# Where the matmul operands lie modulo 512 bytes: moving the weight parts and the stationary arrays of a two-layer decoder trunk apart

## The chip, the core and the metric

The kernel runs on one core of one Trainium2 chip. The metric is the device time of one execution in microseconds (us). Of the kernel before there are three timed runs, and one more execution that the hardware profiler recorded; all numbers on where the time goes come from that one.

## What is computed

The reference is a decoder trunk of two layers over 256 tokens with 2048 features, all in float32. Cut to what matters here:

```python
hn = rms_norm(h, norm_mix[layer])
# layer 0: one input projection (2048 -> 6144), an RG-LRU group and an HGRN2 group, one output projection
# layer 1: q, k, v projection (2048 -> 6144), dilated attention over 16 heads, one output projection
h = h + mix
h = h + squared_relu_mlp(rms_norm(h, norm_mlp[layer]), mlp_w1[layer], mlp_w2[layer])  # 2048 -> 8192 -> 2048
...
return rms_norm(h, final_norm)
```

Nearly all of the arithmetic is matrix products of the 256 tokens with weights that are read once each.

## The kernel before, in words

**Two parts for each operand.** TensorE multiplies in a fast 32-bit format (float32r) that keeps fewer bits than float32. So each operand is split in two: `hi` is the value rounded to that format, `lo` is the rest. A product is three matmuls: hi with hi, hi with lo, lo with hi. The weights come in units of 128 x 2048 float32 (1 MB), by DMA into one of three `raw` buffers. `Weights.split` (L109) has ScalarE make `hi` by a copy (L112) and VectorE make `lo` by a subtraction (L113). There are three buffers each for `hi` and `lo` (pools `whi` and `wlo`, L49 and L50), taken in turn, so that unit n uses buffer n modulo 3, and the three units in flight overlap.

**The activations** are kept split as well, for all of the kernel or a stage of it: `bufa` (normed input, L62), `bufb` (mixed heads or hidden features, L259), `formx` and `formh` (sums and differences of blocks of `bufa` and `bufb`, for products that need seven instead of eight block products, L578 to L594 and L1036).

**The matmul loop.** In `tokens` (L311) and `blocks` (L605) the activation is the stationary operand, 128 x 128, loaded by a weight load (LDWEIGHTS), and a 128 x 512 piece of `hi` or `lo` moves past it. In `direct` (L230), used by layer 0's feature-major projections, it is the other way round: a 128 x 128 block of `hi` or `lo` is stationary, and 256 columns of `bufa` (or `bufb`) move. Every matmul has its own weight load, also where two in a row use the same stationary block. `mm` (L195) ties the matmuls into one fixed order, and `turn` (L198) sets transposes of float32 data into it. Loads of units run two units ahead of the products (`unit`, L185).

**Where arrays lie.** A pool takes a stretch of each partition of SBUF, on top of the pools opened before it; arrays follow each other in the order in which they are first asked for. `xall`, `bufa`, `raw`, `hi`, `lo`, `bufb`, `formx`, `formh`, `s` and `t1` all have sizes that are multiples of 512 bytes per partition, and what lies between them (`tmp`, 2560 bytes) is too. So all of them start at the same place modulo 512 bytes. Pieces that a matmul reads start at multiples of 512 bytes within them (128 or 512 columns of 4 bytes), so the moving and the stationary piece of every float32r matmul start at the same place modulo 512 too. Call the place of the stationary piece minus that of the moving one, modulo 512 bytes, the **distance**: before the change it is 0 throughout. Among the float32 matmuls there are other distances: transposes of `xall`, `y` and `as` by the identity (in `tab_`) have distance 0, those of `ho` have 192; `qT` (stationary) with `kT` has 0, and `xall` (stationary) with `pT` has 320.

Of the kernel before, what the change touches and what calls it, by code (L numbers as in the profile page):

```python
# [10 lines left out]
F32 = mybir.dt.float32  # L11
F32R = mybir.dt.float32r
# [8 lines left out]
P = 128  # L21
# [21 lines left out]
def trunk_kernel(ctx, tc, begin, xtok, cols, tab, masks, pos, fin, w_in, w_gate, w_out, w_qkv, w_o, w1, w2, out):  # L43
    nc = tc.nc
    pool = lambda name, bufs=1, **kw: ctx.enter_context(tc.tile_pool(name=name, bufs=bufs, **kw))
    cst = pool("cst")
    act = pool("act")
    wraw = pool("wraw", 3)
    whi = pool("whi", 3)  # L49
    wlo = pool("wlo", 3)  # L50
    tmp = pool("tmp", 2)
    mixers = ExitStack()
    pmm = pool("pmm", 3, space=PSUM)
# [27 lines left out]
    for step in ORDER.split():  # L81
        src, first, n = where[step[0]]
# [13 lines left out]
                    plan2(src, layer * 64 + q * 16 + 4 * n)  # L96
    at = [0, 0]

    behind, line = {}, []

    class Weights:
        def __init__(self, raw, step=2048, wait=(), follow=False):
            self.raw, self.wait, self.follow = raw, wait, follow
            self.hi = whi.tile([P, 2048], F32R, name="hi")
            self.lo = wlo.tile([P, 2048], F32R, name="lo")
            for at in range(0, 2048, step) if step else ():
                self.split(at, step)

# [95 lines left out]
    def put_off(wait, *fs):  # L204
        later.extend((clock[0] + wait, f) for f in fs)
# [369 lines left out]
    pairs, turned_ = ExitStack(), ExitStack()  # L575

    def open_pairs(layer):
        pool_ = pairs.enter_context(tc.tile_pool(name=f"pair{layer}", bufs=1))  # L578
        return pool_, pool_.tile([P, 4, 2, 512], F32R, name="formh")

    def part_forms(f, k, m, at, src):
# [8 lines left out]
        V.tensor_tensor(s4, a12, s2, OP.add)  # L590

    both = ctx.enter_context(tc.tile_pool(name="both", bufs=1))
    formx = both.tile([P, 4, 2, 512], F32R, name="formx")
    pair, formh = open_pairs(0)  # L594


# [6 lines left out]
    late = []  # L603
# [48 lines left out]
    def pair_forms(forms, k, src, z):  # L652
        h, l = (src[:, k:k + 2, c * S:c * S + S].bitcast(F32) for c in range(2))
        V.tensor_tensor(z.rearrange("p i j c -> p i (j c)"), h, l, OP.add)
        a11, a21, a12, a22 = (z[:, i, j] for i in range(2) for j in range(2))
        combos(a22, a11, a21, a12, a11, a21, a12, a22)
        part_forms(forms, k % 8 // 2, 1, slice(0, 4), z.rearrange("p i j (one c) -> p one (i j) c", one=1))
# [260 lines left out]
    def token_pair(i, c0, ready, raw=()):  # L918
        spare_ = wk.tile([P, 512], F32, name="q0", bufs=1) if not c0 and ATTENTION[:i].count("q") % 2 else None

        def out_(n, j):
            return xres[:, j, c0 + 512 * n:c0 + 512 * n + 512] if spare_ is None or (n, j) != (0, 0) else spare_

        def put(n, j, r=rt):
            def event(bank):
                with urgent():
                    if (n, j) in raw:
                        A.copy(out_(n, j), bank)
                    else:
                        A.activation(out_(n, j), bank, AF.Copy, scale=r[:, j:j + 1])  # L930
            return event

        def add(n, j, bank, r=rt):
            o = out_(n, j)
            with urgent():
                if (n, j) in raw:
                    V.tensor_tensor(o, bank, o, OP.subtract)
                else:
                    V.scalar_tensor_tensor(o, bank, r[:, j:j + 1], o, op0=OP.mult, op1=OP.add)

        def whole(n, j):
            if (n, j) in raw:
                with urgent():
                    A.activation(out_(n, j), out_(n, j), AF.Copy, scale=rt[:, j:j + 1])
            ready(n, j, out_(n, j))

        def final(n, j, bank):
            if (n, j) != (1, 0):
                put(n, j)(bank)
            else:  # L950
                add(n, j, bank)
            if (n, j) != (1, 1):
                whole(n, j)

        def u3(bank):
            add(1, 1, bank, rtn)
            whole(1, 1)

        blocks(w_qkv, 8 * i, 0, feature, formx,
               {"t2": put(1, 0, rtn), "t3": u3}, final)  # L960

    def queries_keys(i, raw=()):
        turned = [wk.tile([P, 4, S], F32, name="qT", bufs=1), wk.tile([P, 4, S], F32, name="kT", bufs=1)]

        def ready(n, j, o):
            t = o.rearrange("p (h c) -> p h c", h=4)
            r = t[:, :, :32].rearrange("p h (two c) -> p h two c", two=2)
            per = lambda a: a[:, j][:, None, :].to_broadcast([P, 4, 16])
            with urgent():
                b = wk.tile([P, 4, 2, 16], F32, name="rb", bufs=2)  # L970
                c = wk.tile([P, 4, 2, 16], F32, name="rc", bufs=2)
                V.tensor_tensor(b[:, :, 0], r[:, :, 1], per(sinT[:, 0]), OP.mult)
                V.tensor_tensor(b[:, :, 1], r[:, :, 0], per(sinT[:, 1]), OP.mult)
                V.tensor_tensor(c, r, cosT[:, j][:, None, None, :].to_broadcast([P, 4, 2, 16]), OP.mult)
                V.tensor_tensor(r, c, b, OP.add)

            def turns():
                p = psc.tile([P, 4, P], F32, name="pl", bufs=2)
                for h in range(4):
                    turn(p[:, h], t[:, h])  # L980
                with urgent():
                    A.copy(turned[n][:, :, j * P:j * P + P], p)

            put_off(WAIT_Q, turns)

        token_pair(i, 0, ready, raw)
        return turned
# [30 lines left out]
    def mix(hd, st):  # L1018
        vs = slice(D // 2 + (hd % 8) * P, D // 2 + (hd % 8) * P + P)
        po = psc.tile([P, S], F32, name="pd" if hd % 2 else "po", bufs=1)  # L1020
        mm(po, xres[:, 0, vs], st[:, :S], start=True, stop=False, skip_group_check=True)
        mm(po[:, P:], xres[:, 1, vs], st[:, S:], start=False, stop=True, skip_group_check=True)
        z = tmp.tile([P, S], F32, name="z")
        with urgent():
            A.copy(z, po)
        split_to(mixed(hd), z)
# [3 lines left out]
    for i, what in enumerate(ATTENTION):  # L1030
        if what == "v":
            token_pair(i, D // 2, lambda *_: None)
            if hd == 16:
                assert len(ready_) == 8
                mixers.close()
                late.append(pairs.enter_context(tc.tile_pool(name="forms1", bufs=1)).tile(  # L1036
                    [P, 8, 512], F32R, name="formh"))
            put_off(2, *(lambda h=h: mix(h, ready_.pop(h)) for h in range(hd - 8, hd)))
            if hd == 8:
                put_off(EARLY, *(lambda k=k: pair_forms(early_forms, k, bufb, wk.tile(  # L1040
                    [P, 512], F32, name="q0", bufs=1).rearrange("p (i j c) -> p i j c", i=2, j=2))
                    for k in range(0, 8, 2)))
        else:
            q, k = queries_keys(i, ((1, 0),) if not i else ())
            for h in range(4):
                put_off(WAIT_Q + 1 + 2 * h, head(hd, q[:, h], k[:, h], WAIT_S))
                hd += 1
# [141 lines left out]
```

## Time and profile before

| | |
|---|---|
| timed runs (3) | median 2133.09 us, 2132.8 to 2133.53 |
| the profiled execution's own time | 2133.06 us |
| its span, first to last instruction | 2131.3 us |
| matmuls, weight loads | 10542 each |
| busy: DVE (VectorE), ACT (ScalarE) | 1788.8 us, 1378.2 us |
| HBM read, mean rate over the span | 482.78 MB, 228 GB/s |

The profile names engines PE (TensorE's matmuls), PEld (its weight loads, which run beside matmuls), DVE, ACT, POOL (GpSimd) and SP (SyncE, which issues most DMAs). A row such as `L196 PE MATMUL p<-hi,bufa 128*128 128x512 f32 x1488 | 482.0, 394 | 0.0` says: line 196 of the kernel, output tile `p`, moving operand `hi`, stationary operand `bufa`, 1488 matmuls, busy 482.0 us in all, 394 ns for one, and 0.0 us of idle time ahead of them. Matmuls overlap in the pipeline, so 394 ns is a latency. What a matmul costs in a stream is the distance in time from its start to the next one's start, and that is read from the timeline or from the chain of work.

### The profile page before, as it was taken

Reading aid. Unit: us, or ns where it says so; the run is one execution under the profiler, and the core shown is the slowest. Engines: PE = TensorE matmul, PEld = TensorE weight load, DVE = VectorE, ACT = ScalarE, POOL = GpSimd, SP = SyncE. Lnnn points to the kernel's source line nnn. Section 1 sums busy time; section 2 is a strip of 40 time slices with the busy share of each in tenths; the row PEclk is TensorE's granted clock in tenths of the full one; section 3 lists DMA queues with packets and bytes.
Section 4 is the critical chain, followed back from the end, with each engine's and each line's share of the span. In section 5 each row is a group of like instructions: output and inputs, shape, how many; then the busy total and the mean of one; then the engine's idle time right before and its main releaser. Section 6 shows DMA issues by size and latency. Waiting matters only on the chain.

```text
span 2131.3 us, 26730 instructions
## 1 busy us (share of the span) xinstructions
PE 2120.9 (100%) x10542; PEld 1797.6 (84%) x10542; DVE 1788.8 (84%) x1962; ACT 1378.2 (65%) x1543; POOL 66.8 (3%) x85
## 2 busy tenths in 40 slices
PE   9999999999999999999999999999999999999998
PEld 8989998888888888888888888888888888888886
DVE  7777888888888888888988797788897888888887
ACT  7445565776476567567666777776756765755764
POOL 0000000000000000000000000000000000000000
PEclk9999999999999999999999999999999999999999
DMA  8444446686777677677887767777767768777773
GB/s 336 162 162 158 161 148 224 206 269 233 227 237 253 230 240 253 227 241 231 270 279 218 241 199 247 254 247 228 246 237 253 236 212 269 238 234 227 271 225 146
DMA packets 69806, 488.71 MB, mean 229 GB/s; under 512 B 7808, under 2 KB 8320, under 8 KB 11952
## 3 DMA queue, kind: packets, MB, share of 16 engines
q1 hardware_dynamic: 58176, 410.96, 51.1%
q0 software_dynamic: 11216, 75.70, 18.3%
q8 instruction: 82, 1.34, 0.3%
q14 instruction: 44, 0.36, 0.0%
q10 hardware_dynamic: 288, 0.34, 0.0%
HBM read 482.78 MB, written 4.19 MB: 228 GB/s over the span
## 4 chain that ended last, share of the span: by engine, by line
PE 99%; DVE 0%; ACT 0%; DMA 0%; issue 0%; ACTq 0%; DVEq 0%; POOLq 0%
PE p L196 62%; PE po L196 14%; PE pd L196 13%; PE pt L196 5%; PE pl L199 2%; PE pl L470 1%; PE pl L196 0%; PE pd L199 0%; DMA ppi<-in_pos 0%; PE pd L454 0%; DVE lo L113 0%; ACT hi L112 0%; PE pl L465 0%; PE po L495 0%; PE po L496 0%
## 5 line engine op out<-in xcount | busy, mean ns | idle before, releaser
L113 DVE TENSOR_TENSOR lo<-raw,hi 128x2048 fp32r<-128x2048 f32 (+2 forms) x397 | 787.1, 1991 | 164.5 <-ACT hi L112 159.4
L112 ACT CAST hi<-raw 128x2048 fp32r<-128x2048 f32 (+2 forms) x397 | 657.3, 1671 | 335.1 <-PE p L196 175.5
L196 PE MATMUL p<-hi,bufa 128*128 128x512 f32 x1488 | 482.0, 394 | 0.0
L196 PE MATMUL p<-hi,bufb 128*128 128x512 f32 x1128 | 363.1, 391 | 0.0
L196 PEld LDWEIGHTS p<-hi,bufa 128*128 128x128 f32 x1488 | 279.2, 188 | 57.3 <-DVE bufa L245 0.5
L113 DVE TENSOR_TENSOR lo<-s,hi 128x2048 fp32r<-128x2048 f32 (+1 forms) x164 | 285.9, 1753 | 28.6 <-ACT hi L112 27.6
L112 ACT CAST hi<-s 128x2048 fp32r<-128x2048 f32 (+1 forms) x164 | 242.7, 1480 | 98.2 <-DVE s L164 54.2
L196 PE MATMUL p<-lo,bufa 128*128 128x512 f32 x744 | 287.6, 390 | 0.2 <-DVE lo L113 0.2
L196 PEld LDWEIGHTS p<-hi,bufb 128*128 128x128 f32 x1128 | 211.7, 188 | 43.7
L196 PE MATMUL p<-lo,bufb 128*128 128x512 f32 x564 | 219.5, 389 | 0.0
L196 PE MATMUL p<-bufa,hi 128*128 128x256 f32 x1024 | 193.2, 287 | 0.0
L196 PEld LDWEIGHTS p<-lo,bufa 128*128 128x128 f32 x744 | 139.9, 188 | 28.0 <-DVE lo L113 0.7
L196 PEld LDWEIGHTS p<-bufa,hi 128*128 128x128 f32 x1024 | 161.2, 191 | 0.2
L196 PE MATMUL p<-bufa,lo 128*128 128x256 f32 x512 | 146.5, 286 | 0.0
L112 ACT CAST hi<-t 128x2048 fp32r<-128x2048 f32 x41 | 78.5, 1914 | 99.6 <-PE p L196 91.1
L113 DVE TENSOR_TENSOR lo<-t,hi 128x2048 fp32r<-128x2048 f32 x41 | 94.0, 2292 | 55.4 <-ACT hi L112 55.0
L196 PEld LDWEIGHTS p<-lo,bufb 128*128 128x128 f32 x564 | 105.9, 188 | 21.5
L196 PE MATMUL p<-hi,formh 128*128 128x512 f32 x368 | 120.7, 391 | 0.0
L196 PE MATMUL p<-hi,formx 128*128 128x512 f32 x352 | 115.9, 390 | 0.0
L196 PE MATMUL po<-hi,bufb 128*128 128x512 f32 x320 | 103.7, 390 | 0.0
L196 PEld LDWEIGHTS p<-bufa,lo 128*128 128x128 f32 x512 | 98.0, 191 | 0.0
L164 DVE TENSOR_TENSOR s<-s,raw 128x1024 f32<-128x1024 f32 x82 | 96.4, 1216 | 0.1
(319 smaller groups left out, 3292.4 us busy)
## 6 DMA issues: line engine op xcount, KB each, us to landing
raw<-in_w SPq DMA_DIRECT2D x224, 1024.0 KB, 6.1
raw<-in_w_in SPq DMA_DIRECT2D x44, 1024.0 KB, 4.8
raw<-in_w_qkv SPq DMA_DIRECT2D x42, 1024.0 KB, 6.9
t<-in_w SPq DMA_DIRECT2D x32, 1024.0 KB, 4.9
t<-in_w POOLq DMA_DIRECT2D x32, 1024.0 KB, 8.7
s<-in_w POOLq DMA_DIRECT2D x17, 1024.0 KB, 8.4
raw<-in_w_out SPq DMA_DIRECT2D x15, 1024.0 KB, 4.8
raw<-in_w_o SPq DMA_DIRECT2D x14, 1024.0 KB, 7.7
```

The source lines that it names most:

```text
L112: a = A.copy(h, w)
L113: v = V.tensor_tensor(l, w, h.bitcast(F32), OP.subtract)
L164: V.tensor_tensor(s, s, held["c"][:, at:at + 1024], OP.add)
L196: chain[:] = [after(T.matmul(*args, **kw), chain)]
L199: chain[:] = [after(T.transpose(out_, in_, ident), chain)]
L470: T.matmul(pl[:, j], kq[:, js], halves(qp[:, js], c, True), start=True, stop=True)
```

## The change

The change moves no instruction and adds none. It adds small arrays that nothing reads or writes, and takes the weight parts from one pool instead of two.

- The pools `whi` and `wlo` become one pool `parts`. Unit n takes `hi{n % 3}` and `lo{n % 3}` there, each with one buffer. Behind each of the three pairs lies an unused array `apart` of 16 floats, 64 bytes.
- `gap2` (48 floats, 192 bytes) lies ahead of `formx`, `gap3` and `gap4` (64 bytes each) ahead of the two homes of `formh`.

Counted from `bufa`'s place modulo 512 bytes, the arrays then lie as follows (before: all at 0):

| array | place after | distance to hi/lo of pair 0, 1, 2, as stationary |
|---|---|---|
| `bufa`, `raw`, `xall` | 0 | `bufa`: 0, 448, 384 |
| `hi0` `lo0`, `hi1` `lo1`, `hi2` `lo2` | 0, 64, 128 | to a moving `bufa`: 0, 64, 128 |
| `bufb` | 192 | 192, 128, 64 |
| `formx`, `s`, `t1` | 384 | `formx`: 384, 320, 256 |
| `formh` | 448 | 448, 384, 320 |

The distance stays 0 only where `bufa` meets pair 0.

```diff
-    whi = pool("whi", 3)
-    wlo = pool("wlo", 3)
+    parts = pool("parts")
...
-    behind, line = {}, []
+    behind, line, turns = {}, [], [0]
...
             self.raw, self.wait, self.follow = raw, wait, follow
-            self.hi = whi.tile([P, 2048], F32R, name="hi")
-            self.lo = wlo.tile([P, 2048], F32R, name="lo")
+            n = turns[0]
+            turns[0] += 1
+            self.hi, self.lo = (parts.tile([P, 2048], F32R, name=f"{part}{n % 3}") for part in ("hi", "lo"))
+            if n < 3:
+                parts.tile([P, 16], F32, name=f"apart{n}")
...
         pool_ = pairs.enter_context(tc.tile_pool(name=f"pair{layer}", bufs=1))
+        pool_.tile([P, 16], F32, name="gap3", bufs=1)
...
     both = ctx.enter_context(tc.tile_pool(name="both", bufs=1))
+    both.tile([P, 48], F32, name="gap2", bufs=1)
...
-                late.append(pairs.enter_context(tc.tile_pool(name="forms1", bufs=1)).tile(
+                forms1 = pairs.enter_context(tc.tile_pool(name="forms1", bufs=1))
+                forms1.tile([P, 16], F32, name="gap4", bufs=1)
+                late.append(forms1.tile(
                     [P, 8, 512], F32R, name="formh"))
```

## The prediction

> **What bounds the kernel now.** I read the page first: busy times, the clock row, and the shares of the chain of work that ended last.
>
> ```profile
> span 2131.3 us, 26730 instructions
> ...
> PE 2120.9 (100%) x10542; PEld 1797.6 (84%) x10542; DVE 1788.8 (84%) x1962; ACT 1378.2 (65%) x1543; POOL 66.8 (3%) x85
> ...
> PEclk9999999999999999999999999999999999999999
> ...
> PE 99%; DVE 0%; ACT 0%; DMA 0%; issue 0%; ACTq 0%; DVEq 0%; POOLq 0%
> ```
>
> TensorE works from end to end, at the full granted clock, and the chain is 99% its own. Next comes the view of who waited for whom, for the engines that make the weight parts.
>
> ```profile
> ACT hi L112 <- PE p L196: 269.1, 142, 4.3
> DVE lo L113 <- ACT hi L112: 242.0, 300, 3.8
> ```
>
> ScalarE waits for TensorE to give a buffer back (269.1 us in 142 waits), VectorE waits for ScalarE. The makers are ahead; TensorE sets the time. So only the distance from one matmul's start to the next one's can change the time by much. The chain in order of time gives it for long streams (start, length, count):
>
> ```profile
> 552.07 13.60 PE p L196 x60
> ...
> 2089.95 13.60 PE p L196 x60
> ```
>
> 13.60 us / 60 = 226.7 ns for a matmul of 512 moving columns, the same at both ends of the kernel. For 256 columns the timeline of layer 0's projections gives a stretch of 21 matmuls:
>
> ```profile
> 60.03 0.40 PE L196 MATMUL p<-bufa,hi 128*128 128x256 f32 x2
> ...
> 62.55 0.40 PE L196 MATMUL p<-bufa,hi 128*128 128x256 f32 x2
> ```
>
> (62.55 - 60.03) / 21 = 120.0 ns. So 256 more columns cost 226.7 - 120.0 = 106.7 ns, and a fixed 226.7 - 2 x 106.7 = 13.3 ns is left per matmul, for both lengths. This fixed part is all that the change can win; nothing else on TensorE's path depends on where arrays lie.
>
> **The change, part by part.** It moves places and no work: no DMA, cast, subtraction or matmul is added or dropped, and no queue is passed. Three things could cost or bring something.
>
> *1. The turn of the buffers.* Unit n still waits for unit n - 3, as with three buffers of one name. I cost it at nothing. What hides it is ScalarE's lead above: it would have to lose more than its waits for TensorE, up to 4.3 us each, before TensorE noticed. The bounds: if the new names gave another order of instructions, TensorE could wait a few times; by that longest wait, one or two of these are 4 to 9 us, and as TensorE hardly waits now, less than nothing is no gain. I take 0.
>
> *2. ScalarE and VectorE read and write at other places.* Their instructions have slack, as shown. Taken: 0.
>
> *3. The distance between moving and stationary piece.* Each matmul runs while the next one's stationary block is loaded. Before, the two reads start at the same place modulo 512 bytes, always; after, only `bufa` with pair 0 does. How many matmuls is that? The groups by shape and tile:
>
> ```profile
> L196 PE MATMUL p<-hi,bufa 128*128 128x512 f32 x1488 | 482.0, 394 | 0.0
> L196 PE MATMUL p<-hi,bufb 128*128 128x512 f32 x1128 | 363.1, 391 | 0.0
> ...
> L196 PE MATMUL p<-bufa,hi 128*128 128x256 f32 x1024 | 193.2, 287 | 0.0
> ...
> L196 PE MATMUL p<-hi,formh 128*128 128x512 f32 x368 | 120.7, 391 | 0.0
> L196 PE MATMUL p<-hi,formx 128*128 128x512 f32 x352 | 115.9, 390 | 0.0
> ...
> L196 PE MATMUL pt<-lo,formh 128*128 128x512 f32 x8 | 3.1, 389 | 0.0
> ```
>
> The 36 groups between the first and the last of these that hold `hi` or `lo` add up to 9,588 matmuls: 4,824 with `bufa`, 2,700 with `bufb`, 1,056 with `formx`, 1,008 with `formh`. A third of `bufa`'s meet pair 0 and keep distance 0. The distance changes for 9,588 - 4,824 / 3 = 7,980.
>
> What a changed distance costs, the trace doesn't show for float32r, as all of these are at distance 0. The bounds:
>
> - *Best:* the whole fixed part is the two reads in each other's way and goes away: 7,980 x 13.3 ns = 106 us less.
> - *Worst:* the fixed part grows. The nearest row is a stretch that follows four transposes, where the stream is out of its usual step:
>
> ```profile
> 379.45 0.60 PE L199 MATMUL pl<-tab__199,xall 128*128 128x128 f32 x4
> 379.81 0.48 PE L196 MATMUL po<-hi,formh 128*128 128x512 f32 x1
> 380.12 0.40 PE L196 MATMUL po<-lo,formh 128*128 128x512 f32 x1
> ...
> 382.44 0.39 PE L196 MATMUL po<-hi,formh 128*128 128x512 f32 x1
> ```
>
>   Ten matmuls from 380.12 to 382.44 take 2.32 us, 232.0 ns each, 5.3 ns over the settled 226.7. Same columns, same arrays; only the step of load and stream differs. If the new distances kept the stream out of step throughout: 7,980 x 5.3 ns = 42 us more.
> - *Nearest rows with another distance:* float32 matmuls. Transposes by the identity load a stationary block at distance 0 (`y`, `xall`) or 192 (`ho`); `qT` with `kT` is at 0, `xall` with `pT` at 320:
>
> ```profile
> L199 PE MATMUL pl<-tab__199,y 128*128 128x128 f32 x256 | 33.1, 272 | 0.0
> ...
> L199 PE MATMUL pl<-tab__199,xall 128*128 128x128 f32 x152 | 22.6, 272 | 0.0
> ...
> L196 PE MATMUL pl<-kT,qT 128*128 128x256 f32 x32 | 9.6, 380 | 0.0
> ...
> L508 PE MATMUL pt<-tab__199,ho 128*128 128x128 f32 x16 | 4.1, 273 | 0.0
> ...
> L196 PE MATMUL po<-pT,xall 128*128 128x256 f32 x16 | 4.7, 377 | 0.0
> ```
>
>   272 and 272 ns at distance 0, 273 at 192; 380 at distance 0, 377 at 320. A distance of 0 costs 1 ns less in one pair and 3 ns more in the other.
>
> I take 0 for the distance, as the rows with another distance are nearest to it and disagree in sign. A fixed part that is equal for 256 and 512 columns also looks like a cost of changing over from one stationary block to the next. I keep both ends for the range.
>
> One page of the Trainium skill speaks against any gain: "TensorE: Matmul & The Clock Gate", section "Part 2: What happens when you issue a matmul", says that TensorE has two independent read ports into SBUF, so that loading the next weights takes nothing from the running matmul; by that rule the sum is 0. The trace can't show it, as it has no float32r matmul at another distance.
>
> *The sum:* the profiled execution's own 2133.06 us (span 2131.3 and 1.8 around it) + 0 + 0 + 0 = **2133.1 us**, which is also the median of the three runs within 0.03 us.
>
> **The rivals.**
>
> *Slower: the stream doesn't settle.* For: the interval does depend on how load and stream stand to each other (232.0 against 226.7 ns), and the settled step was found at distance 0, one constant distance from matmul to matmul and from unit to unit. After, the distance jumps with each pair, that is every 12 to 24 matmuls, about as long as settling took above. Against: nothing shows that places and not only times make the step. Price: 2133.1 + 42 = 2175 us if no stretch at a new distance settles; if it settles half-way through each unit, 2154. It decides for slower as soon as the mean interval at new distances is over 227.2 ns (0.2% of 2133, 4.3 us, over 7,980).
>
> *Faster: the fixed part is a collision at equal places.* For: each matmul pays 13.3 ns beyond its columns, and `kT` with `qT`, at distance 0, takes 3 ns more than `pT` with `xall`. Against: the transposes show nothing, and a load and a stream that read at different speeds pass through all distances anyhow. Price: 2133.1 - 106 = 2027 us in full, 2080 for half of it. Nothing else would be late then: VectorE's 1788.8 us of work still fit under 2027. The same page's section "Back-to-back issue gap" gives columns / 2.4 + 2.5 ns for a matmul, 215.8 for 512 columns, where this trace measures 226.7. If the 10.9 ns between them were the collision, the gain would be 7,980 x 10.9 ns = 87 us and the time 2046; that is an estimate from the page's figure.
>
> *The change does nothing:* arrays that nobody uses might be given no space, or the reads may be arbitrated by something coarser or finer than 64 bytes. Then the time is 2133.1 too, and it belongs to the forecast.
>
> **How the numbers follow.** 0.2% is 4.3 us, about what a measurement of this kernel can tell from no change. Within 0.2%: 0.40, the likeliest, so the predicted time is 2133.1 us, and its own range is 2129 to 2137. Slower: 0.34, as the trace proves that the step of load and stream matters and that other steps than the settled one cost more; its times are spread from 2138 to 2185. Faster: 0.26, from 2027 to 2128. As the cases of both signs hold more than half, the range reaches into both: to 2085 (a gain of 48 us, somewhat under half of the best; 0.09 lies below) and to 2180 (a little over the full price of the unsettled stream; 0.07 lies above).
>
> **What would show it.** In the profile of the changed kernel, the chain in order of time has the streams of 60 matmuls: 13.60 us means the forecast, about 13.9 the unsettled stream, 13.0 or less the collision. The mean would not say which distance does it: the intervals at `bufa` with pair 0 must stay at 226.7 ns whatever the others do, and if a distance matters, the stretches of one pair with one array differ from each other in the timeline. If ScalarE's waits for TensorE have shrunk while TensorE shows idle time at `lo` or `hi`, the turn of the buffers was costed wrongly. The prediction is wrong if the streams of 60 have another length; it is right for a wrong reason if gains at some distances cancel losses at others.

## The result, and the profile after

The changed kernel takes 2160.56 us (median of 4 runs, 2160.49 to 2161.39), the kernel before 2132.95 us (4 runs): a ratio of 1.0132, interval 1.012 to 1.0144, 27.6 us more. The page of the changed kernel:

```profile
span 2159.6 us, 26730 instructions
...
PE 2148.1 (99%) x10542; PEld 1796.2 (83%) x10542; DVE 1789.8 (83%) x1962; ACT 1377.9 (64%) x1543; POOL 66.8 (3%) x85
...
PEclk9999999999999999999999999999999999999999
...
PE 98%; ACT 1%; DVE 1%; DMA 0%; issue 0%; SPq 0%; ACTq 0%
```

As many instructions as before, the same work on DVE and ACT within 1 us, the same clock, and the span 28.3 us longer. TensorE still makes up nearly the whole chain. ScalarE's waits for TensorE have grown a little, from 269.1 us; the makers of the weight parts are still ahead (the view of waits of the changed kernel):

```profile
ACT hi L114 <- PE p L198: 283.4, 160, 4.3
DVE lo L115 <- ACT hi L114: 263.6, 322, 3.9
```

So TensorE's matmuls follow each other more slowly. The chain of the changed kernel in order of time (start, length, count), where 60 matmuls took 13.60 us before:

```profile
596.75 13.90 PE p L198 x60
...
766.53 13.71 PE p L198 x60
...
1066.47 13.97 PE p L198 x60
```

They take 228.5 to 232.8 ns each now, and differ from stream to stream. The timeline shows what they go by. Units take pairs 0, 1, 2 in turn, so each stretch has one pair and one array. Starts at the ends of three stretches in the changed kernel (columns: start, length, what):

```profile
383.43 0.40 PE L198 MATMUL p<-lo,bufb 128*128 128x512 f32 x1
...
388.55 0.39 PE L198 MATMUL p<-hi,bufb 128*128 128x512 f32 x1
388.78 0.39 PE L198 MATMUL p<-hi,formh 128*128 128x512 f32 x1
...
391.58 0.39 PE L198 MATMUL p<-hi,bufb 128*128 128x512 f32 x1
...
396.85 0.39 PE L198 MATMUL p<-hi,bufb 128*128 128x512 f32 x1
```

- `bufb` with pair 1, distance 128: 22 matmuls in 5.12 us, 232.7 ns each.
- `formh` with pair 2, distance 320: 12 in 2.80 us, 233.3 ns.
- `bufb` with pair 0, distance 192: 23 in 5.27 us, 229.1 ns.

Layer 0's matmuls of 256 columns, where `bufa` moves past `hi` or `lo`, went the other way at one distance:

```profile
60.03 0.40 PE L198 MATMUL p<-bufa,hi 128*128 128x256 f32 x2
...
63.51 0.28 PE L198 MATMUL p<-bufa,lo 128*128 128x256 f32 x1
...
68.45 0.28 PE L198 MATMUL p<-bufa,lo 128*128 128x256 f32 x1
```

Pair 0, distance 0: 29 matmuls in 3.48 us, 120.0 ns as before. Pair 1, distance 64: 42 in 4.94 us, 117.6 ns.

Taken over all float32r matmuls, each one's time from start to next start in the changed kernel minus that of the same matmul in the kernel before, added up by distance modulo 256:

| distance | 512 columns: matmuls, us more | 256 columns: matmuls, us more |
|---|---|---|
| 0 | 1416, 1.6 | 576, -0.2 |
| 64 | 1560, 9.9 | 432, -1.3 |
| 128 | 2640, 13.6 | 624, -0.6 |
| 192 | 2339, 5.5 | none |

The sum is 30.6 - 2.1 = 28.5 us; all other matmuls give -0.1 us, so this is the whole of the span's 28.3 but for rounding. Why modulo 256, and whether distance or something that goes with it does this, is what the experiments are for.

### The profile page after: what moved, and what is told of

It is laid out like the page before. It is cut to its first block, busy times and chain, and to the rows that moved or that the text cites. A ratio compares the mean times of both kernels' runs of the same rounds, so it can differ in the third digit from the quotient of the medians.

```text
span 2159.6 us, 26730 instructions
## 1 busy us (share of the span) xinstructions
PE 2148.1 (99%) x10542; PEld 1796.2 (83%) x10542; DVE 1789.8 (83%) x1962; ACT 1377.9 (64%) x1543; POOL 66.8 (3%) x85
## 4 chain that ended last, share of the span: by engine, by line
PE 98%; ACT 1%; DVE 1%; DMA 0%; issue 0%; SPq 0%; ACTq 0%
PE p L198 62%; PE po L198 14%; PE pd L198 13%; PE pt L198 5%; PE pl L201 2%; PE pl L472 1%; PE pl L198 0%; DMA first<-in_begin 0%; PE pd L201 0%; PE pd L456 0%; ACT hi L114 0%; DVE lo L115 0%; ACT L227 0%; DVE xc L549 0%; ACT gi L227 0%
## 5 line engine op out<-in xcount | busy, mean ns | idle before, releaser
L198 PE MATMUL p<-hi,bufb 128*128 128x512 f32 x1128 | 367.7, 394 | 0.0
L198 PE MATMUL p<-hi,formx 128*128 128x512 f32 x352 | 117.6, 395 | 0.0
```

Of the source, the lines that this page charges most:

```text
L198: chain[:] = [after(T.matmul(*args, **kw), chain)]
```

## The experiments

Theory A: the time from one matmul to the next is set by the distance between the stationary and the moving piece. Theory B, the prediction's slower rival: distances as such cost nothing, but a jump of the distance unsettles the stream. All kernels below are one edit of the kernel before or of the changed one. Intervals that are called means are of all matmuls of a kind in a trace, those next to float32 matmuls (over 260 ns, or over 160 ns at 256 columns) left out.

**Other steps** (`e1_probe32`), an edit of the changed kernel:

```diff
-                parts.tile([P, 16], F32, name=f"apart{n}")
+                parts.tile([P, 8], F32, name=f"apart{n}")
...
-    both.tile([P, 48], F32, name="gap2", bufs=1)
+    both.tile([P, 16], F32, name="gap2", bufs=1)
```

> The same edit with half of the steps: pairs at 0, 32, 64 bytes, bufb at 96, formx at 160, formh at 224. Theory A (the interval between matmuls is a function of the distance between the stationary and the moving piece modulo 256 bytes, whatever the arrays): at distances 64, 128 and 192 the same intervals as in the changed kernel, 233.4, 232.2 and 229.5 ns, now with other arrays; the new distances 32, 96, 160 and 224 lie between their neighbours, about 230, 233, 231 and 228 ns, and the time is about 2155 us. Theory B (a jump of the distance from pair to pair unsettles the stream, whatever the distance): jumps as often as in the changed kernel, so about 2160 us and intervals that do not depend on the distance.

2167.29 us (2 runs), against 2132.8 for the kernel before: slower than either theory said. Means with `bufb` at 64: 233.2 ns; with `formx` at 128: 232.9; with `formh` at 192: 230.0, so other arrays at the known distances have the known intervals within 0.6 ns. The new ones do not lie between their neighbours: 233.0 at 32, 233.8 at 96, 233.8 at 160, 233.1 at 224. Distance matters, and 0 is a narrow dip.

**One constant distance of 64** (`e2_all64`), an edit of the kernel before:

```diff
+    pool("ahead").tile([P, 48], F32, name="ahead")
     whi = pool("whi", 3)
     wlo = pool("wlo", 3)
+    pool("behind").tile([P, 16], F32, name="behind")
```

> The kernel before with 192 bytes ahead of the weight parts and 64 behind them: every stationary array now lies at one and the same distance, 64 bytes modulo 256, from every pair, so nothing jumps. Theory A: 233.4 ns in place of 227.2 for some 7825 matmuls of 512 columns, 48 us more, less up to 6 us in layer 0's matmuls of 256 columns: about 2177 us, 2168 to 2185. Theory B: no jumps, so 2133 us.

2177.56 us, ratio 1.021 (1.0195 to 1.0225). In the chain of this kernel all such streams take 14.00 or 14.01 us:

```profile
556.74 14.00 PE p L198 x60
598.74 14.00 PE p L198 x60
```

14.00 / 60 = 233.3 ns, with no jump anywhere. Theory B falls as the only cause: a constant distance of 64 costs more than the changed kernel's jumps.

**A distance of 256** (`e3_bufa256`): as above, with 64 floats ahead of `whi` and none behind.

> The kernel before with 256 bytes ahead of the weight parts: bufa now lies at distance 256 from every pair, bufb, formx and formh stay at 0. Theory A (period 256): 2133 us, within 4 us. Rival C (period 512, so that 256 is a distance like the others, with 2 to 6 ns more for bufa's 3203 intervals): 2139 to 2153 us. Theory B: 2133 us.

2133.21 us, ratio 1.0002 (0.9992 to 1.0012), streams as in the kernel before:

```profile
550.99 13.60 PE p L197 x60
```

The period is 256 bytes, not 512. It also shows that what moved with `hi` and `lo` (their distance to `raw`, 256 bytes) does no harm.

**The gaps alone** (`e4_gaps`): the changed kernel without the steps between pairs.

```diff
     parts = pool("parts")
+    pool("behind").tile([P, 48], F32, name="behind")
     tmp = pool("tmp", 2)
...
-            if n < 3:
-                parts.tile([P, 16], F32, name=f"apart{n}")
```

> The changed kernel without the steps between the pairs: all three pairs at 0, bufb at 192, formx at 384, formh at 448 as there. The distance is constant for each array. Theory A: bufb 2580 x 2.5 ns, formx 1042 x 5.3 ns, formh 1000 x 2.5 ns, 14.5 us in all: about 2147.5 us, 2143 to 2152, with bufa at its old interval. Theory B: only the changes from array to array are left, 2133 to 2138 us.

2147.11 us, ratio 1.0067 (1.0052 to 1.0082), 14.3 us more where theory A had 14.5 us. Modulo 512, `hi`, `lo` and `raw` lie here where they were, and of the operands only the stationary arrays have moved. The streams, `bufb` at 192 and `formh` at 448:

```profile
552.50 13.73 PE p L197 x60
```

13.73 / 60 = 228.8 ns. `bufa`, at distance 0 throughout, has a mean of 228.1 here and 227.5 in the kernel before.

**The pairs alone** (`e8_pairs`): the changed kernel without the three gaps, and with an `apart2` that puts `bufb` back to 0.

```diff
-                parts.tile([P, 16], F32, name=f"apart{n}")
+                parts.tile([P, 16 if n < 2 else 96], F32, name=f"apart{n}")
...
-        pool_.tile([P, 16], F32, name="gap3", bufs=1)
...
-    both.tile([P, 48], F32, name="gap2", bufs=1)
...
-                forms1.tile([P, 16], F32, name="gap4", bufs=1)
```

> The other half of the change: pairs at 0, 64 and 128 as in the changed kernel, bufb, formx and formh back at 0. Theory A: every array now meets distances 0, 192 and 128 in turn, 2.8 ns more on average for some 7825 matmuls, 22 us, less 2.6 us in the 256-column ones: about 2152 us, 2148 to 2157, so that the two halves, 14.3 us (gaps alone) and this, add up to more than the whole's 27.6. Rival F (the halves cost each for itself): 27.6 - 14.3 = 13.3 us, 2146 us.

2157.42 us, ratio 1.0112 (1.0097 to 1.0128), against 2133.21: 24.2 us more, at the upper edge of theory A. The two halves add up to 38.5 us where the whole costs 27.6, so rival F falls: a distance is a difference, and moving both sides can bring them back together. What theory A missed by 5 us is in the third of the matmuls that are at distance 0. With `bufb` they take 229.1 ns here and 227.0 ns in the kernel before. The timeline shows why; this unit of `bufb` with pair 0 starts at 554.12, behind one of `formh` at another distance:

```profile
554.35 0.40 PE L198 MATMUL p<-lo,bufb 128*128 128x512 f32 x1
...
556.43 0.39 PE L198 MATMUL p<-lo,bufb 128*128 128x512 f32 x1
...
559.15 0.39 PE L198 MATMUL p<-lo,bufb 128*128 128x512 f32 x1
```

Nine matmuls in 2.08 us, 231.1 ns each, then 12 in 2.72 us, 226.7 ns each: coming from another distance, the stream needs part of the unit to settle. So the jumps do cost something, at distance 0.

**The source of the parts** (`e7_raw64`), an edit of the kernel before:

```diff
+    pool("ahead").tile([P, 16], F32, name="ahead")
     wraw = pool("wraw", 3)
+    pool("behind").tile([P, 48], F32, name="behind")
```

> The kernel before with raw moved: 64 bytes ahead of the raw buffers and 192 behind them, so that raw lies 64 bytes (modulo 256) from the hi and lo that are made of it, while hi, lo and all stationary arrays stay at distances of 0 or 256 from each other. Theory A: 2133 us, within 4 us. Rival D (the places that ScalarE and VectorE read and write while TensorE reads are what counts): another time, 10 us or more away, as in the changed kernel.

2132.78 us, ratio 0.9999 (0.999 to 1.0008), and the streams stay:

```profile
551.49 13.60 PE p L198 x60
592.29 13.60 PE p L198 x60
```

Rival D falls for the casts' source. ScalarE's casts do not feel the places either; here they are in the kernel before (first row), in this one (second) and in the changed one (third), with minimum, median and maximum in ns after the count:

```profile
L112 ACT CAST hi<-raw x397: 604/1912/1927, 21.5 to 2106.3; 128x2048 fp32r<-128x2048 f32 x144, 128x1024 fp32r<-128x1024 f32 x54, 128x512 fp32r<-128x512 f32 x1
```

```profile
L114 ACT CAST hi<-raw x397: 604/1907/1922, 21.5 to 2106.1; 128x2048 fp32r<-128x2048 f32 x144, 128x1024 fp32r<-128x1024 f32 x54, 128x512 fp32r<-128x512 f32 x1
```

```profile
L114 ACT CAST hi<-raw x397: 603/1906/1930, 21.7 to 2134.3; 128x2048 fp32r<-128x2048 f32 x144, 128x1024 fp32r<-128x1024 f32 x54, 128x512 fp32r<-128x512 f32 x1
```

**Under 32 bytes** (`e6_fine`): each pair is one array, and within it pair 1 starts 16 bytes on and pair 2, which lies 32 bytes further on, another 8.

```diff
-            self.hi, self.lo = (parts.tile([P, 2048], F32R, name=f"{part}{n % 3}") for part in ("hi", "lo"))
-            if n < 3:
-                parts.tile([P, 16], F32, name=f"apart{n}")
+            both_, o = parts.tile([P, 4096 + (0, 8, 8)[n % 3]], F32R, name=f"hi{n % 3}"), (0, 4, 2)[n % 3]
+            self.hi, self.lo = both_[:, o:o + 2048], both_[:, o + 2048:o + 4096]
...
-        pool_.tile([P, 16], F32, name="gap3", bufs=1)
...
-    formx = both.tile([P, 4, 2, 512], F32R, name="formx")
+    formx = both.tile([P, 4096 + 8], F32R, name="formx")[:, 4:4100].rearrange("p (a b c) -> p a b c", a=4, b=2)
...
-                forms1.tile([P, 16], F32, name="gap4", bufs=1)
```

> Distances under 32 bytes: pairs at 0, 16 and 40 bytes, bufb at 64, formx at 16, formh at 32, so that distances of 16, 24, 48, 216, 232, 240 and 248 bytes come up beside 0, 32 and 64; hi and lo of a pair share one array. Theory A: each distance has an interval of its own; if it rises steadily from 226.7 ns at 0 to 233 at 32, then 16 and 240 give about 230, and the time is about 2155 us. Rival E (only whole blocks of 32 bytes or more count): 16 and 24 give 226.7 as 0 does, 48 gives 233 as 32 does.

2172.1 us (one run), 17 us above what theory A had. The timeline, with `formh` and pair 1 at a distance of 272 bytes, which is 16 modulo 256:

```profile
399.42 2.95 PE L197 MATMUL po<-hi,formh 128*128 128x512 f32 x12
...
402.21 2.97 PE L197 MATMUL p<-hi,bufb 128*128 128x512 f32 x12
```

(402.21 - 399.42) / 12 = 232.5 ns. Rival E falls, and so does the steady rise: the mean is 233.0 at 16 bytes already, 234.0 at 24, and on the other side 231.6 at 240 and 233.2 at 248.

This run also has a case at distance 0 that stays slow. `formx` and pair 1 both lie at 16 modulo 256 here; one of their units:

```profile
468.92 2.94 PE L197 MATMUL po<-hi,formx 128*128 128x512 f32 x12
471.69 0.39 PE L197 MATMUL p<-hi,bufa 128*128 128x512 f32 x1
```

12 matmuls in 2.77 us, 230.8 ns each; the mean of all of them is 230.7, where `bufa` with pair 0, both at 0, has 228.1 in the same run. So distance 0 isn't always quick. Whether the place of 16 bytes does it, or units of 12 matmuls are too short to settle behind such neighbours, isn't shown.

**lo apart from hi** (`e9_lo64`), an edit of the kernel before, meant to find out which of two reads it is:

```diff
     whi = pool("whi", 3)
+    pool("ahead").tile([P, 16], F32, name="ahead")
     wlo = pool("wlo", 3)
+    pool("behind").tile([P, 48], F32, name="behind")
```

> The kernel before with lo 64 bytes (modulo 256) further on than hi, all else at 0. In layer 0's projections the order is hi past the first half of the columns, hi past the second, lo past the first. Theory A1 (what counts is the moving piece against the block that is being loaded for the next matmul): the short interval, below 118 ns, is that of the second matmul, beside which lo is loaded; theory A2 (against the block that the matmul itself uses): that of the third, which uses lo. In the matmuls of 512 columns one in three meets distance 192: up to 2.5 ns for a third of 7825, 6.5 us, so 2133 to 2140 us in all.

2166.9 us, ratio 1.0161 (1.0144 to 1.0178): 34.1 us more, outside of what was expected. Two matmuls of three are at distance 0 here and should have kept 226.7 ns. The timeline shows hi, hi, lo in turn:

```profile
383.89 0.39 PE L198 MATMUL p<-lo,bufb 128*128 128x512 f32 x1
384.12 0.62 PE L198 MATMUL p<-hi,bufb 128*128 128x512 f32 x2
...
388.06 0.40 PE L198 MATMUL p<-lo,formh 128*128 128x512 f32 x1
```

18 matmuls in 4.17 us, 231.7 ns each; over the whole trace, 231.8 ns at distance 0 and 232.1 at 192. Here a matmul at distance 0 isn't quick, as one of the two before it was at 192; with the unit of the pairs run that settles after some ten matmuls, this says that the distances before count as well. So theory A in its simple form falls, and becomes theory G: the sequence of distances counts. A1 and A2 stay undecided: the three intervals of layer 0's triple are 118.1, 117.8 and 118.2 ns, all below 120.

**The control for it** (`e11_lo256`): 64 floats ahead of `wlo`, nothing behind.

> The control for the run in which lo lay 64 bytes off hi and all intervals, those at distance 0 too, rose to some 232 ns: lo 256 bytes further on than hi, all else as there. Theory G (what counts is the sequence of distances modulo 256, and only one that stays at 0 lets the stream settle at 226.7 ns): 2133 us, within 4 us. Rival H (hi and lo at different places modulo 512 is enough): about 2167 us, as there.

2133.17 us, ratio 1.0 (0.9991 to 1.001), as theory G has it:

```profile
551.76 13.60 PE p L197 x60
```

**One constant distance of 128** (`e12_all128`): 32 floats ahead of `whi`, 32 behind `wlo`.

> All stationary arrays at one distance, 128 modulo 256, from every pair (128 bytes ahead of the parts, 128 behind), so that the settled interval is seen without any jump. Theory G: a constant distance other than 0 does not settle at 226.7 ns; as in the changed kernel some 232.4 ns, 41 us more for 7825 matmuls, less 2 us in the 256-column ones: about 2172 us, 2165 to 2178. Theory B (jumps alone cost): 2133 us.

2176.08 us, ratio 1.0202 (1.0185 to 1.0219), as theory G has it. The streams, in two kinds:

```profile
558.14 13.94 PE p L198 x60
...
1831.17 14.00 PE p L198 x60
```

232.3 and 233.3 ns. Without any jump, this distance doesn't settle at 226.7 ns.

**A faster version** (`e5_layer0`). Layer 0's 256-column matmuls gain from a distance of 64. They are the only place where `bufa` moves, and that stage's input can have a place of its own in a `bufa` that is 256 bytes larger:

```diff
-    bufa = act.tile([P, KB, 2 * S], F32R, name="bufa")
+    home = act.tile([P, KB * 2 * S + 64], F32R, name="bufa")
+    bufa, bufl = (home[:, at:at + KB * 2 * S].rearrange("p (k s) -> p k s", k=KB) for at in (0, 48))
...
-        p = project(w_in, b, bufa)
+        p = project(w_in, b, bufl)
```

(and so for all of layer 0's projections and the split of its input).

> A version meant to be faster: the kernel before, with layer 0's normed input kept 192 bytes further on than bufa's place in the other stages (in the same, 256 bytes larger array), so that in layer 0's projections the stationary hi or lo lies 64 bytes behind the moving piece, modulo 256. Theory A: some 1469 intervals of 256 columns go from 119.8 ns to about 116, 5.6 us less; some 384 of 512 columns there go to 229.4, 1 us more; all else stays: about 2128.3 us, 2125 to 2131. Theory B (only jumps count): 2133 us.

2128.81 us against 2133.21, ratio 0.998 (0.9971 to 0.9988): faster than both kernels by a little, as theory A has it. Its timeline has two stretches

```profile
58.22 0.28 PE L197 MATMUL p<-bufa,lo 128*128 128x256 f32 x1
...
67.06 0.28 PE L197 MATMUL p<-bufa,lo 128*128 128x256 f32 x1
...
312.79 0.28 PE L197 MATMUL p<-bufa,lo 128*128 128x256 f32 x1
...
324.45 0.28 PE L197 MATMUL p<-bufa,lo 128*128 128x256 f32 x1
```

of 78 matmuls in 8.84 us, 113.3 ns each, and of 99 in 11.66 us, 117.8 ns each. Shape, arrays and distance are the same in both. Of the 37 unbroken stretches of 18 or more such matmuls, the first six of each left out, 16 have a mean of 113.3 or 113.4 ns and 21 one of 117.7 or 117.8; the mean over all is 116.2 ns. So at distance 64 there are two settled steps, and a stretch keeps the one that it falls into; what decides between them isn't shown.

**A look beside 64** (`e10_probe0`): the version above with `bufl` at 208 bytes, and with the changed kernel's one pool of pairs, here 32 bytes apart. Against the version above, cut to the places:

```diff
-    bufa, bufl = (home[:, at:at + KB * 2 * S].rearrange("p (k s) -> p k s", k=KB) for at in (0, 48))
+    bufa, bufl = (home[:, at:at + KB * 2 * S].rearrange("p (k s) -> p k s", k=KB) for at in (0, 52))
...
+            if n < 2:
+                parts.tile([P, 8], F32, name=f"apart{n}")
```

> A look for a better distance in layer 0's projections: its input 208 bytes on, pairs at 0, 32 and 64, so that 256-column matmuls meet distances of 48, 80 and 112; bufb, formx and formh at 64. Theory A: the intervals of 512 columns are those known for 0, 32, 64, 192 and 224, about 29 us more in all, so about 2157 us. If 48, 80 or 112 gives less than the 116.1 ns of distance 64 in 256-column matmuls, a better version is to be had by it; a rise on both sides of 64 means that 64 is the place.

2161.75 us (one run), 5 us above the expectation. The 256-column means are 119.0 ns at 48, 119.1 at 80 and 118.4 at 112: none is below the 116.2 of distance 64.

This run settles one more question: is it the distance, or does an array have to start at a multiple of 256? `bufb` and pair 2 both lie at 64 modulo 256 here:

```profile
364.08 0.39 PE L199 MATMUL p<-lo,bufb 128*128 128x512 f32 x1
...
368.84 0.39 PE L199 MATMUL p<-lo,bufb 128*128 128x512 f32 x1
```

21 matmuls in 4.76 us, 226.7 ns each, as in the kernel before. With neither array at a multiple of 256, distance 0 still settles at the quick step.

## Why the time came out as it did, point by point

**What bounds the kernel** was read rightly: the time lies in the intervals between matmuls, and the sum of their changes is the span's 28.3 us but for rounding.

**Part 1 and part 2**, the turn of the buffers and the places that ScalarE and VectorE use, were costed at 0 and cost 0: gaps alone move nothing that these engines write in the weight units and cost what the matmuls' intervals say; moving `raw` changed nothing.

**Part 3 is the step that failed.** The time came 27.6 us above the forecast of no change. Part 3 took 0 for a changed distance, from float32 matmuls whose distances of 0 and 192 or 320 differed by 1 and 3 ns, and read a fixed part that is equal at 256 and 512 columns as a cost of changing blocks. The runs show that float32r matmuls of 512 columns go from 226.7 to 229.0 ns (192), 232.3 to 233.3 (128) and 233.3 (64) at constant distances, up to 6.6 ns. The float32 rows weren't a fair stand-in, and they were read by the wrong column: 272, 380 and 377 ns are latencies, not times from start to start. In the changed kernel the float32r latency moved by as little as those did, from 391 to 394 ns for `bufb`:

```profile
L198 PE MATMUL p<-hi,bufb 128*128 128x512 f32 x1128 | 367.7, 394 | 0.0
```

while the interval of `bufb`'s matmuls went from 227.0 ns to 229.5, 232.1 and 233.3 at its three distances. Beside the 13.3 ns in question, 3 ns was no reason for 0. That the shorter shape has its own best distance (64, where 0 is best for 512 columns) speaks against one changing-over cost as well. Its count was also a little high: modulo 256 the distance changed for 7,596 matmuls and not 7,980. The 6,539 of 512 columns among them (with a start behind them) took 28.9 us more, 4.4 ns each, against the 5.3 of the worst case. The bounds around the value, 106 us less and 42 more, held.

The range held because it was drawn out over the slower rival, which had a chance of 0.34, and not because the forecast was near. By the prediction's own signs the forecast fails: the streams of 60 took 13.71 to 13.97 us and not 13.60, and `bufa` with pair 0, which was to stay at 226.7 ns, has a mean of 228.3. The gain at 256 columns, 2.1 us, cancelled a small part of the loss.

**The slower rival** is what came, with 27.6 us between its two prices of 21 and 42 us. Its mechanism was half right. Right: the stream settles into a step that depends on how load and stream stand to each other, and leaving distance 0 keeps it out of the best one. Wrong, as far as it laid the cost to the jumps: constant distances of 64 and 128 cost 44.8 and 42.9 us with no jump from pair to pair. Jumps add a cost mainly at distance 0, some 2 ns per matmul when they come with each unit (229.1 in the pairs run against 227.0) and nearly 5 ns when they come within each triple of matmuls (231.8 against 227.2 over all arrays); at 192 they add 0.6 to 1.0 ns (229.0 constant, 229.6 and 230.0 with jumps).

**The faster rival**, a collision at equal places, had the sign wrong for 512 columns. For 256 columns it was right in sign: the mean went from 119.8 to 116.2 ns at distance 64.

**The page of the Trainium skill** that stood against a gain, "TensorE: Matmul & The Clock Gate", section "Part 2: What happens when you issue a matmul", says that loading the next weights takes no SBUF read bandwidth from the running matmul. For float32r, the 0 that was drawn from it doesn't come out: moving only the stationary arrays (the gaps alone) costs 14.3 us, and the interval ranges from 226.7 to 234 ns by places alone. Whether it is read bandwidth that is lost, no run shows. The same holds for a sentence of "SBUF — State Buffer", section "Who interferes with whom", that TensorE never waits on anyone, as far as it is taken to include TensorE's own two reads.

**What stays open.** The runs show that the interval depends on the distance modulo 256 and on the distances of the matmuls before. They also show that this isn't all: at one constant distance, 256 columns settle at 113.3 or 117.8 ns (64) and 512 columns at 232.3 or 233.3 (128), and where both pieces lie at 16 modulo 256, distance 0 stays at 230.7. That the two reads of TensorE collide in some unit of SBUF is the natural reading, but only argued. The rows give one hint: the weight loads beside matmuls of 256 columns take 191 ns on average in the kernel before and 188 in the run with one constant distance (192 bytes for this shape), and those beside 512 columns take 188 in both. Which block matters, the one in use or the one being loaded, is undecided, as is why distance 0 settles well at 512 columns and 64 at 256.

## What to carry to other kernels

Place is a parameter of a matmul: where the moving and the stationary array start modulo 256 bytes moved this kernel by 2% with not one instruction changed, so when arrays are added or resized, keep these distances as they were, or measure them. Change one side at a time and read the intervals in one trace by distance: three pairs against four arrays gave up to ten distances in one run. And a row of another format (float32 here) is a weak stand-in for a cost that no row shows, and a latency is a weak stand-in for an interval; how far the row is from the case belongs in the range.

## What the runs showed that was not expected

- The dip at distance 0 is narrow: 226.7 ns settled at 0 and 256, but means of 233.0 at 16 and 233.2 at 248, only 8 bytes below 256.
- A matmul's interval depends on those before it: at distance 0 the mean for `bufb` is 227.0 ns if all are at 0, 229.1 if the distance changes with each unit, and 231.9 if it changes within each triple of matmuls.
- For 256 columns, distance 0 is the slowest of those tried (119.8 ns on average; 119.1 at 80, 118.4 at 112, 117.8 at 192, 116.2 at 64), and distance 64 has two settled steps, 113.3 and 117.8 ns.
- The ends of the settled steps are equally far apart for both shapes: 226.7 and 233.3 ns at 512 columns, 113.3 and 120.0 at 256.
